# The sums for the adaLN gates in another stage, the third product's first operands split at another place, and residual rows and results by other times and queues

## Chip, cores, metric

The kernel runs on one core of one Trainium2 chip. The metric is the device time of one execution in microseconds, as the median of several; a profile shows one execution, taken by itself.

## What is computed

One step of a one-layer encoder over 2048 prompt tokens and 32 sample tokens of width 1024, all in fp32. The part of the reference that matters here:

```
mod = silu(c) @ w_ada + b_ada
shift, scale, gate = split(mod, 3)
h = rms_norm(x, norm_g) * (1 + scale) + shift
... = h @ w_in                       # q, k, v, za, index, u, bg, cg, zb, ga, gb
o = sparse_attention(...)            # top 256 keys of each query
a_out = (o * silu(za)) @ w_pa
b_out = (bg * y_conv * silu(zb)) @ w_pb
merged = sigmoid(ga) * a_out + sigmoid(gb) * b_out
y = x + gate * (merged @ w_out)
```

`gate` is one row of 1024 for the prompt and one for the sample tokens: a product of silu(c) with the last third of w_ada (`w_g` here, eight blocks of 128x1024, 512 KB each), done by VectorE as sums along a row.

## The kernel before

Products of fp32 numbers are made of two halves each: `split` casts an operand on ScalarE (ACT) to its high part, and VectorE (DVE) subtracts that from it for the low part (L173, L174); TensorE then does three matmuls. `wh`/`wl` are the parts of weights, `xh`/`xl` those of the other operand. The program is written for a tile framework; a scheduler sets the order of instructions on each engine from a simulated time, and `keep_in_program_order` binds single instructions to the order of the code. Each engine then executes strictly in that order, SyncE's (SP) queue of DMAs included.

The attention runs from about 1785 to 2363 us. Beside it goes a list of side work, `sum_steps`: sums of blocks of weights and pieces of the conv branch for the output stage, each with a cost, of which so many are done after each attention block as the block's share of the total asks for. At the end of that list stands `gates` (L1189): for each of the two rows it loads the row `c_d` to all partitions, loads the eight blocks of w_g (L1203, through the tiles `wq`), multiplies and sums each on DVE (L1206, `cgt`), adds the bias (L1210), and stores both results to `g_d` in DRAM (L1212), 4 KB each in pieces of 4 bytes.

The output stage `outputs` (L1451) does 64 products in the order of STEPS. For each of three groups of tokens (384, 384 and 256 + 16 columns) come b0 to b6 (conv branch), a0 to a6 (attention branch) and m0 to m6 (w_out): seven products of a Strassen-like scheme, where a matrix product of 2x2 blocks costs seven products of halves and some additions. A b or a product (`feature_step`, L1614 to L1616) has 48 matmuls of 384 (272) columns, an m product (`token_step`, L1678 to L1680) 72 of 256; in group 2 `sample_part` (L1636 to L1638) adds the sample tokens, whose split operands are `smh` and `sml`. After the matmuls of product n the code splits the operands of n+1 (`w_split`, `x_split`) and loads weights (`rw`, two of 512 KB) and pieces (`xq`, 768 KB) for n+3. Products 0 to 2 of each seven are copied out of PSUM by ACT (L1571), 3 to 6 added on DVE (L1575) and multiplied by the branch's gates `g` (L1583); a finished block of branch a is added to that of branch b (L1591), and so is an operand of the m products. `sums_a` (L1527 to L1530) makes differences of these blocks: q00 and t1, of which t1 is the operand of m1, and q01, that of m2. `ENDS` gives the block that products 3 to 6 finish; that of a6 is the operand of m3.

The products m3 to m6 load the residual rows into tiles `x` (L1670, six buffers, 128 KB a load) at their own start, multiply by the adaLN gate (L1686), add the rows (L1687) and store the result (L1689), all loads and stores on SP's queue. The gate tile itself is loaded at the stage's start from `g_d` (L1552).

## Time and profile before

| | |
|---|---|
| median of 3 runs | 2910.27 us (2905.02 to 2916.78) |
| profiled execution | 2908.65 us, its span 2906.9 us |
| PE busy in the span | 2788.8 us (96%), mean granted clock 0.986 |
| DVE, ACT, POOL busy | 2208.4 (76%), 1488.3 (51%), 924.2 us (32%) |
| DMA | 561.36 MB, mean 193 GB/s |
| output stage | from 2363.66 us on |

TensorE (PE) is the engine to look at: outside its busy time lie some 118 us of the span, and the rows below show which of them stand around the places that the change touches. In lists of waits a line reads "engine line waited for: us in total, times, longest us". In timelines the bracket at a line's end is the idle time of that engine before the instruction and what ended it. In windows, "PEclk" is the granted TensorE clock as a share of full speed, "DMA share" the busy share of the 16 DMA engines.

### The profile page before, as it was taken

To read this page: it belongs to the slowest core of one execution; us is meant where nothing else is said; L and a number is where in the kernel's file an instruction comes from. 1 tells how busy PE (TensorE), PEld (TensorE's weight loads), DVE (VectorE), ACT (ScalarE), POOL (GpSimd) and SP (SyncE) were. 2 spreads that over 40 slices of the span, in tenths; PEclk is the share of its full clock that TensorE was granted. 3 is DMA by queue.
4 is the path that set the end of the run, shared out by engine and by line. 5 is a ranking of instruction groups with operands and counts; after the bars stand their busy time and mean duration, and the time that the engine had idled before them with its cause. 6 is when DMAs were issued, how large, how long until landed. Compare 5 with 4: busy or idle time off the path is not lost. (4 is left out here: it accounts for less than half of the span.)

```text
span 2906.9 us, 53619 instructions
## 1 busy us (share of the span) xinstructions
PE 2788.8 (96%) x18925; PEld 2691.5 (93%) x18925; DVE 2208.4 (76%) x4948; ACT 1488.3 (51%) x2861; POOL 924.2 (32%) x1364
## 2 busy tenths in 40 slices
PE   7999999999999999999999999899999979999998
PEld 4999998999989999999999999889999879999997
DVE  5666576767664779999997878787777856888787
ACT  4434334666545665565553444555555544444453
POOL 2324223645544522222232222675544210000000
PEclk9999999999999999999999999999999999999999
DMA  7525567545554556555667666576555568596684
GB/s 255 179 92 184 158 218 242 191 147 171 167 179 161 164 178 204 186 180 185 208 212 226 203 223 170 143 209 179 170 161 158 169 194 301 189 292 220 216 296 142
DMA packets 469040, 561.36 MB, mean 193 GB/s; under 512 B 175584, under 2 KB 357272, under 8 KB 467736
## 3 DMA queue, kind: packets, MB, share of 16 engines
q1 hardware_dynamic: 464056, 553.57, 60.5%
q10 hardware_dynamic: 4704, 4.26, 0.4%
q8 instruction: 151, 2.47, 0.4%
q14 instruction: 129, 1.06, 0.1%
HBM read 373.34 MB, written 190.66 MB: 194 GB/s over the span
## 5 line engine op out<-in xcount | busy, mean ns | idle before, releaser
L975 PE MATMUL pm<-bh,wo 128*128 128x352 f32 (+1 forms) x2352 | 754.0, 322 | 2.7 <-ACT ev L987 1.2
L976 PE MATMUL pm<-bl,wo 128*128 128x352 f32 (+1 forms) x2352 | 753.2, 320 | 0.1
L977 PE MATMUL pm<-bh,wo 128*128 128x352 f32 (+1 forms) x2352 | 752.4, 321 | 0.0
L975 PEld LDWEIGHTS pm<-bh,wo 128*128 128x128 f32 x2352 | 442.7, 188 | 9.8 <-ACT ev L987 1.9
L976 PEld LDWEIGHTS pm<-bl,wo 128*128 128x128 f32 x2352 | 442.9, 188 | 5.7 <-DVE bl L174 0.6
L977 PEld LDWEIGHTS pm<-bh,wo 128*128 128x128 f32 x2352 | 442.0, 188 | 4.9 <-issue 0.5
L174 POOL TENSOR_TENSOR wo<-wr,wo 128x512 fp32r<-128x512 f32 x140 | 208.3, 1488 | 579.0 <-ACT wo L173 562.1
L745 PE MATMUL pm<-wh,hhi 128*128 128x256 f32 (+4 forms) x1088 | 309.5, 287 | 9.5 <-DVE sm L719 4.3
L746 PE MATMUL pm<-wl,hhi 128*128 128x256 f32 (+4 forms) x1088 | 307.5, 285 | 0.8 <-DVE wl L174 0.8
L747 PE MATMUL pm<-wh,hlo 128*128 128x256 f32 (+4 forms) x1088 | 306.4, 285 | 0.5 <-DVE hlo L174 0.5
L173 ACT CAST wh<-rw 128x1024 fp32r<-128x1024 f32 x128 | 134.1, 1051 | 211.9 <-PE ps L1615 83.3
L234 DVE SCALAR_TENSOR_TENSOR sc<-pi,wi,sc 128x512 f32<-128x512 f32 (+3 forms) x287 | 192.1, 670 | 55.0 <-ACT pi L230 51.6
L174 DVE TENSOR_TENSOR wl<-rw,wh 128x1024 fp32r<-128x1024 f32 x128 | 156.4, 1224 | 92.8 <-ACT wh L173 92.5
L173 ACT CAST th<-pt 128x512 fp32r<-128x512 f32 (+1 forms) x288 | 155.5, 562 | 137.0 <-PE pt L1380 124.0
L230 ACT ACTIVATE pi<-pi 128x512 f32<-128x512 f32 (+3 forms) x328 | 164.4, 516 | 118.8 <-PE pi L229 113.5
L1614 PE MATMUL ps<-xh,wh 128*128 128x384 f32 (+1 forms) x672 | 215.0, 323 | 9.7 <-ACT xh L173 5.6
L1615 PE MATMUL ps<-xl,wh 128*128 128x384 f32 (+1 forms) x672 | 216.1, 323 | 3.6 <-DVE xl L174 3.6
L1616 PE MATMUL ps<-xh,wl 128*128 128x384 f32 (+1 forms) x672 | 214.5, 322 | 0.7 <-DVE wl L174 0.7
L745 PEld LDWEIGHTS pm<-wh,hhi 128*128 128x128 f32 (+1 forms) x1088 | 200.0, 185 | 12.6 <-issue 5.1
L174 DVE TENSOR_TENSOR tl<-pt,th 128x512 fp32r<-128x512 f32 (+1 forms) x288 | 183.8, 656 | 35.2 <-ACT th L173 34.2
L746 PEld LDWEIGHTS pm<-wl,hhi 128*128 128x128 f32 (+1 forms) x1088 | 200.3, 185 | 2.4 <-issue 0.9
L747 PEld LDWEIGHTS pm<-wh,hlo 128*128 128x128 f32 (+1 forms) x1088 | 199.6, 184 | 1.8 <-DVE hlo L174 0.7
(307 smaller groups left out, 7151.2 us busy)
## 6 DMA issues: line engine op xcount, KB each, us to landing
u<-u_d SPq DMA_DIRECT2D x112, 520.0 KB, 4.4
wr<-in_w_f_dram SPq DMA_DIRECT2D x84, 512.0 KB, 3.8
rw<-o_d SPq DMA_DIRECT2D x72, 512.0 KB, 5.4
u_d<-ev SPq DMA_DIRECT2D x168, 176.0 KB, 2.2
rw<-in_w_q_dram SPq DMA_DIRECT2D x56, 512.0 KB, 5.3
wr<-in_w_t_dram SPq DMA_DIRECT2D x32, 512.0 KB, 4.7
xa_d<-a SPq DMA_DIRECT2D x64, 256.0 KB, 4.0
s_d<-ws SPq DMA_DIRECT2D x56, 256.0 KB, 2.9
```

The source lines that it names most:

```text
L173: S.copy(hi, src)
L174: (eng or V).tensor_tensor(lo, src, hi.bitcast(F32), ALU.subtract)
L234: V.scalar_tensor_tensor(sc[:n, o:o + w], pi[:n, :w], wi[:n, b, h:h + 1], sc[:n, o:o + w], ALU.mult, ALU.add)
L745: T.matmul(pm[:n, :ncol], a, hi[:, kt, :ncol], start=(kt == 0), stop=False)
L746: T.matmul(pm[:n, :ncol], a, lo[:, kt, :ncol], start=False, stop=False)
L747: T.matmul(pm[:n, :ncol], b_, hi[:, kt, :ncol], start=False, stop=(kt == KT - 1))
L975: T.matmul(ps[:, :tb], wh[:, kt, :], bh[:, kt, :tb], start=(first and kt == 0), stop=False, **more)
L976: T.matmul(ps[:, :tb], wh[:, kt, :], bl[:, kt, :tb], start=False, stop=False, **more)
L977: T.matmul(ps[:, :tb], wl[:, kt, :], bh[:, kt, :tb], start=False, stop=(kt == 3), **more)
L1614: T.matmul(ps[:, :tb], wh[:, kt, wc], xh[:, kt, :tb], start=(first and kt == 0), stop=False, **more)
L1615: T.matmul(ps[:, :tb], wh[:, kt, wc], xl[:, kt, :tb], start=False, stop=False, **more)
L1616: T.matmul(ps[:, :tb], wl[:, kt, wc], xh[:, kt, :tb], start=False, stop=(kt == 3), **more)
```

## The change

`gates` and its place at the end of the side list are gone. In the output stage the gate tile first holds the two rows of `c_d`. Halves of w_g's blocks (128x512, 256 KB, each loaded once) come by GpSimd's queue into pairs of the `x` tiles, three pairs ahead, and DVE sums each half with both rows (32 instructions of 128x512), three halves behind each of the products b0 to b2 and a0 to a2 of group 0. After a2 `gate_rows` adds the bias, stores to `g_d` and loads the gate tile from it on SP, as before. The operands of m0 are split behind a5, together with those of a6. The addition of a6's block and the difference q01 come behind m0, and the instructions around m1 are bound to the code's order. Residual rows are loaded one product ahead, and results are stored by GpSimd's queue, but for the last product's.

```diff
-        def gates():
...
-                    tc.keep_in_program_order(V.tensor_tensor_reduce(st["w"], st["w"], st["c"], 1.0, 0.0, ALU.mult, ALU.add, cgt[:, v, i:i + 1]))
...
-        return steps + gates()
+        return steps
...
+            def osplit(hi, lo, src, keep):
+                S.copy(hi, src)
+                ins = V.tensor_tensor(lo, src, hi.bitcast(F32), ALU.subtract)
+                if keep:
+                    tc.keep_in_program_order(ins)
...
-                V.tensor_tensor(t1[:, :, :tb], q11, q00, ALU.subtract)
-                V.tensor_tensor(q01, q11, q01, ALU.subtract)
+                tc.keep_in_program_order(V.tensor_tensor(t1[:, :, :tb], q11, q00, ALU.subtract))
+
+            def sums_c(g):
+                tb = GROUPS[g][1]
+                q01, q11 = [quads[g, "m", k][:, :, :tb] for k in QS[1:3]]
+                tc.keep_in_program_order(V.tensor_tensor(q01, q11, q01, ALU.subtract))
...
-            load(gate, g_d.rearrange("(o v) d -> o v d", o=1).broadcast_to([P, 2, D]))
+            cgt = oc.tile([P, 2, KT, 2], F32, name="cgt")
+            gws = {}
+
+            def gate_load(u):
+
+                if u < 2 * KT:
+                    gws[u] = xtile(), xtile()
+                    G.dma_start(gws[u][0], w_g[u // 2, :, 512 * (u % 2):512 * (u % 2) + 512])
+
+            def gate_sum(u):
+                w, t = gws.pop(u)
+                i, h = u // 2, u % 2
+                for v in range(2):
+                    V.tensor_tensor_reduce((t, w)[v], w, gate[:, v, 512 * h:512 * h + 512], 1.0, cgt[:, v, i, 0:1] if h else 0.0, ALU.mult, ALU.add,
+                                           cgt[:, v, i, h:h + 1])
+
+            def gate_rows():
+                g1 = cgt[:, :, :, 1]
+                V.scalar_tensor_tensor(g1, vecs[:, 16:24].unsqueeze(1).to_broadcast([P, 2, KT]), 0.25, g1, ALU.mult, ALU.add)
+                for v in range(2):
+                    store(g_d[v].rearrange("(k p) -> p k", p=P), cgt[:, v, :, 1])
+                load(gate, g_d.rearrange("(o v) d -> o v d", o=1).broadcast_to([P, 2, D]))
...
-                if j > 2:
+                if j > 2 and (jb, j) != ("a", 6):
                     gated(g, jb, j)
...
+            def rows_load(n):
+                g, jb, j = STEPS[n]
+                if jb == "m" and 2 < j < 7:
+                    resid[n] = [xtile() for _ in range(GROUPS[g][1] // P)]
+                    for i, x in enumerate(resid[n]):
+                        for q in range(2):
+                            load(x[64 * q:64 * q + 64], x_prompt[0][rows(n, i, q)])
...
-                                store(y_p[0][rows(i, q)], o[64 * q:64 * q + 64])
+                                (G.dma_start if n + 1 < len(STEPS) else store)(y_p[0][rows(n, i, q)], o[64 * q:64 * q + 64])
...
+            for v in range(2):
+                load(gate[:, v], c_d[v:v + 1].broadcast_to([P, D]))
+            for u in range(3):
+                gate_load(u)
+            units = list(range(2 * KT))
             for n, (g, jb, j) in enumerate(STEPS):
                 (token_step if jb == "m" else feature_step)(n)
                 wop.pop(n)
-                w_split(n + 1)
-                x_split(n + 1)
+                m0 = jb == "a" and j == 6
+                if not m0:
+                    w_split(n + 1)
+                    x_split(n + 1)
+                if jb == "a" and j == 5:
+
+                    w_split(n + 2)
+                    x_split(n + 2)
                 w_load(n + 3)
                 x_load(n + 3)
-                if jb == "a" and j == 6:
+                if n + 1 < len(STEPS):
+                    rows_load(n + 1)
+                if g == 0 and jb != "m" and j < 3:
+                    for u in units[:3]:
+                        gate_sum(u)
+                        gate_load(u + 3)
+                    units[:3] = []
+                    if jb == "a" and j == 2:
+                        gate_rows()
+                if m0:
                     sums_a(g)
+                if jb == "m" and j == 0:
+                    sums_c(g)
+                    gated(g, "a", 6)
```

On SP's queue, from the attention's last store of `a` on, before: loads of w_g, b3's weights (`rw_29615`, `rw_29617`), branch gates `g`, the store of the sums and residual rows `x` stand in one row.

```order
L1203 DMA wq_28882<-in_w_g_dram 128x1024
L1403 DMA xa_d<-a_29476 128x8x64
L1203 DMA wq_28885<-in_w_g_dram 128x1024
L1488 DMA rw_29615<-in_w_q_dram 128x2x512
L1514 DMA g_29621<-gb_d 128x4x768
L1212 DMA g_d<-cgt 128x8x1 x2
L1514 DMA g_29694<-gb_d 128x4x768
L1670 DMA x_30872<-in_x_prompt_dram 64x512 x2
L1488 DMA rw_29617<-in_w_q_dram 128x2x512
L1670 DMA x_30875<-in_x_prompt_dram 64x512
L1488 DMA rw_29688<-o_d 128x2x512
L1670 DMA x_30875<-in_x_prompt_dram 64x512
```

The same place after:

```order
L1369 DMA xa_d<-a_29420 128x8x64
L1706 DMA gate<-c_d 128x1024 x2
L1486 DMA g_29591<-gb_d 128x4x768
L1486 DMA g_29679<-gb_d 128x4x768
L1460 DMA rw_29570<-in_w_q_dram 128x2x512
L1460 DMA rw_29572<-in_w_q_dram 128x2x512
L1480 DMA xq_29750<-xb_d 128x4x384
L1460 DMA rw_29658<-o_d 128x2x512
L1480 DMA xq_29843<-xb_d 128x4x384
L1460 DMA rw_29660<-o_d 128x2x512
L1480 DMA xq_29922<-xa_d 128x4x384
```

The rows `c_d` and the branch gates now come first, b3's weights (`rw_29570`, `rw_29572`) stand together, and nothing of w_g, `g_d` or `x` is left there. The store of the sums and the gate's load now stand further down, between the two halves of a6's weights (`rw_30392`, `rw_30394`) and the first residual rows:

```order
L1460 DMA rw_30309<-o_d 128x2x512
L1660 DMA x_30902<-in_x_prompt_dram 64x512 x2
L1660 DMA x_30903<-in_x_prompt_dram 64x512
L1460 DMA rw_30392<-in_w_q_dram 128x2x512
L1660 DMA x_30903<-in_x_prompt_dram 64x512
L1548 DMA g_d<-cgt 128x8x1 x2
L1460 DMA rw_30394<-in_w_q_dram 128x2x512
L1660 DMA x_31017<-in_x_prompt_dram 64x512 x2
L1660 DMA x_31018<-in_x_prompt_dram 64x512
L1549 DMA gate<-g_d 128x2048
L1660 DMA x_31018<-in_x_prompt_dram 64x512
```

On DVE at the change from attention to output stage, before (the last three sums of w_g; `wl_29604` and `wl_29677` are weights of b1 and b2):

```order
L1398 TENSOR_TENSOR a_29476<-z_29474,po_29345 128x256
L1206 ISA wq_28882,cgt<-wq_28882,wq_28689 128x1024
L1206 ISA cgt 128x1
L174 TENSOR_TENSOR wl_29677<-rw_29542,wh_29676 128x1024
L1206 ISA wq_28885,cgt<-wq_28885,wq_28689 128x1024
L1206 ISA cgt 128x1
L1210 SCALAR_TENSOR_TENSOR cgt<-vecs,cgt 128x16
L174 TENSOR_TENSOR wl_29604<-rw_29536,wh_29603 128x1024
L174 TENSOR_TENSOR wl_29608<-rw_29538,wh_29607 128x1024
L174 TENSOR_TENSOR xl_29612<-xq_29534,xh_29611 128x1536
L174 TENSOR_TENSOR xl_29685<-xq_29540,xh_29684 128x1536
```

The same place after, where the sums (L1541) begin behind the splits of b1 and stand between those of b2 and b3:

```order
L1364 TENSOR_TENSOR a_29420<-z_29418,po_29289 128x256
L1443 TENSOR_TENSOR wl_29559<-rw_29480,wh_29558 128x1024
L1443 TENSOR_TENSOR wl_29563<-rw_29482,wh_29562 128x1024
L1443 TENSOR_TENSOR xl_29567<-xq_29478,xh_29566 128x1536
L1443 TENSOR_TENSOR wl_29647<-rw_29486,wh_29646 128x1024
L1541 ISA x_29493,cgt<-x_29492,gate 128x512
L1541 ISA cgt 128x1
L1443 TENSOR_TENSOR xl_29655<-xq_29484,xh_29654 128x1536
L1541 ISA x_29492,cgt<-x_29492,gate 128x512
L1541 ISA cgt 128x1
L1443 TENSOR_TENSOR wl_29651<-rw_29488,wh_29650 128x1024
L1443 TENSOR_TENSOR xl_29743<-xq_29574,xh_29742 128x1536
```

No sum stands ahead of b1's splits any more; the first stands ahead of the split of b2's piece (`xl_29655`).

On DVE between the last gates of group 0's a6 and the split of m3's operand, before (`xl_30680` is m1's, split from t1 = `xq_30589`; `ob_29708` is a6's block):

```order
L1591 TENSOR_TENSOR ob_29635<-ob_29635,oa_30157 128x1536
L1583 SCALAR_TENSOR_TENSOR oa_30230<-g_30216,ps_30111 128x384
L174 TENSOR_TENSOR wl_30676<-rw_30517,wh_30675 128x1024
L1527 TENSOR_TENSOR ob_29559<-ob_29635,ob_29559 128x1536
L1591 TENSOR_TENSOR ob_29708<-ob_29708,oa_30230 128x1536
L174 TENSOR_TENSOR wl_30764<-rw_30584,wh_30763 128x1024
L1529 TENSOR_TENSOR xq_30589<-ob_29858,ob_29559 128x1536
L1530 TENSOR_TENSOR ob_29635<-ob_29858,ob_29635 128x1536
L174 TENSOR_TENSOR xl_30864<-ob_29708,xh_30863 128x1536
L174 TENSOR_TENSOR wl_30768<-rw_30586,wh_30767 128x1024
L174 TENSOR_TENSOR xl_30680<-xq_30589,xh_30679 128x1536
```

The same place after (`xl_30708` is m1's, from t1 = `xq_30618`; `ob_29693` is a6's block):

```order
L1588 TENSOR_TENSOR ob_29605<-ob_29605,oa_30172 128x1536
L1580 SCALAR_TENSOR_TENSOR oa_30254<-g_30240,ps_30111 128x384
L1499 TENSOR_TENSOR ob_29514<-ob_29605,ob_29514 128x1536
L1501 TENSOR_TENSOR xq_30618<-ob_29858,ob_29514 128x1536
L1443 TENSOR_TENSOR wl_30700<-rw_30557,wh_30699 128x1024
L1443 TENSOR_TENSOR wl_30704<-rw_30559,wh_30703 128x1024
L1443 TENSOR_TENSOR wl_30794<-rw_30613,wh_30793 128x1024
L1443 TENSOR_TENSOR xl_30708<-xq_30618,xh_30707 128x1536
L1506 TENSOR_TENSOR ob_29605<-ob_29858,ob_29605 128x1536
L1588 TENSOR_TENSOR ob_29693<-ob_29693,oa_30254 128x1536
L1443 TENSOR_TENSOR wl_30798<-rw_30615,wh_30797 128x1024
L1443 TENSOR_TENSOR xl_30802<-ob_29605,xh_30801 128x1536
```

The addition of a6's block (L1591, now L1588), q01 (L1530, now L1506) and the splits for m3 moved from the front of m1's split to behind it.

## Rows read from the trace of the kernel before

**Rows 1.** The list of waits, TensorE only, from 2300 to 2907 us: who waited for whom, us in total, times, longest.

```profile
PE ps L1678 <- ACT xh L173: 8.5, 2, 4.2
PE ps L1614 <- ACT xh L173: 5.6, 2, 3.9
PE ps L1614 <- ACT ob L1571: 4.0, 1, 4.0
PE po L1388 <- DVE a L1398: 3.7, 2, 2.2
PE ps L1615 <- DVE xl L174: 3.6, 1, 3.6
PE ps L1636 <- ACT smh L173: 2.2, 1, 2.2
...
PE ps L1638 <- DVE sml L174: 1.8, 1, 1.8
```

**Rows 2.** Windows of the output stage: busy us (x instructions) of each engine, granted clock, DMA share, GB/s.

```profile
2370.00:2390.00 20.00, 14.65 (x72) 14.01 (x71) 11.49 (x11) 10.20 (x12) 0.00 (x0) 0.83 0.75 167
2400.00:2420.00 20.00, 16.13 (x71) 15.84 (x70) 8.97 (x10) 5.88 (x8) 0.00 (x0) 0.76 1.05 319
2510.00:2520.00 10.00, 6.28 (x30) 5.99 (x31) 8.59 (x6) 4.89 (x5) 0.00 (x0) 0.66 1.00 380
2690.00:2710.00 20.00, 15.61 (x108) 15.11 (x107) 14.03 (x10) 9.99 (x12) 0.00 (x0) 0.83 0.63 224
2830.00:2840.00 10.00, 10.00 (x81) 9.84 (x80) 10.00 (x23) 4.82 (x7) 0.00 (x0) 1.00 0.35 117
2840.00:2860.00 20.00, 15.93 (x113) 14.55 (x113) 17.62 (x25) 9.14 (x12) 0.00 (x0) 0.83 0.42 131
```

**Rows 3.** Windows of the attention's end and of group 0's b and a products, the same columns.

```profile
2300.00:2330.00 30.00, 25.95 (x190) 23.40 (x188) 25.76 (x49) 17.12 (x25) 6.13 (x13) 1.00 0.70 225
2330.00:2363.50 33.50, 29.15 (x227) 27.72 (x228) 21.99 (x39) 14.02 (x22) 5.74 (x13) 0.95 0.65 219
2414.70:2442.60 27.90, 27.82 (x146) 27.85 (x147) 26.81 (x37) 11.79 (x11) 0.00 (x0) 0.90 0.92 316
2442.60:2467.60 25.00, 25.00 (x146) 25.00 (x145) 13.48 (x12) 14.94 (x21) 0.00 (x0) 1.00 0.85 311
2467.60:2500.90 33.30, 33.30 (x195) 33.30 (x195) 32.13 (x42) 12.97 (x13) 0.00 (x0) 1.00 0.42 135
```

**Rows 4.** The instructions of line L1206, the sums over w_g: durations in ns (min/median/max), and what their engine waited for ahead of them (us, times).

```profile
L1206 DVE CUSTOM_DVE_ANT_0 wq<-wq,wq x16: 1214/1226/1279, 2277.1 to 2372.9; 128x1024 f32<-128x1024 f32 x16
...
  DMA wq<-in_w_g_dram: 11.7, 7
```

**Rows 5.** The list of waits, SP's queue only, from 2270 to 2425 us.

```profile
SPq L1203 <- DVE cgt L1206: 24.4, 7, 4.7
```

**Rows 6.** Timeline of SP's queue, start and duration of an issue.

```profile
2374.33 3.73 SPq L1212 DMA_DIRECT2D g_d<-cgt  x2
...
2380.93 4.14 SPq L1670 DMA_DIRECT2D x<-in_x_prompt_dram  x2
```

**Rows 7.** The view of the DMAs from 2360 to 2400 us: GB/s in 40 slices of one microsecond, then groups of issues with KB of each and median us from issue to landing.

```profile
GB/s 208 281 295 0 0 41 319 175 219 41 180 328 176 141 198 315 397 403 297 169 33 0 6 44 46 52 25 68 114 350 390 415 324 219 305 258 236 268 252 240
...
g<-gb_d SPq DMA_DIRECT2D x2, 1536.0 KB, 16.1
wq<-in_w_g_dram SPq DMA_DIRECT2D x3, 512.0 KB, 3.6
xq<-xb_d SPq DMA_DIRECT2D x2, 768.0 KB, 11.2
...
g_d<-cgt SPq DMA_DIRECT2D x2, 4.0 KB, 12.3
```

**Rows 8.** Timeline of ACT in the stage's start.

```profile
2397.16 1.04 ACT L173 CAST wh<-rw 128x1024 fp32r<-128x1024 f32 x1 [10.38 <-DMA rw<-in_w_q_dram]
```

**Rows 9.** Timeline of DVE ahead of group 0's m1.

```profile
2504.46 1.75 DVE L1591 TENSOR_TENSOR ob<-ob,oa 128x1536 f32<-128x1536 f32 x1
...
2507.27 1.75 DVE L1529 TENSOR_TENSOR xq<-ob,ob 128x1536 f32<-128x1536 f32 x1
```

**Rows 10.** Timeline of ACT at the same place.

```profile
2509.24 1.47 ACT L173 CAST xh<-ob 128x1536 fp32r<-128x1536 f32 x1 [0.73 <-PE ps L1679]
...
2512.05 1.47 ACT L173 CAST xh<-xq 128x1536 fp32r<-128x1536 f32 x1
```

**Rows 11.** Groups of DVE's instructions by line and shape over the whole span: count, busy us, mean ns of one, idle time before them.

```profile
L174 DVE TENSOR_TENSOR wl<-rw,wh 128x1024 fp32r<-128x1024 f32 x128 | 156.4, 1224 | 92.8 <-ACT wh L173 92.5
...
L1355 DVE CUSTOM_DVE_ANT_0 s<-ps,mk 128x512 f32<-128x512 f32 x32 | 21.8, 688 | 10.9 <-PE ps L1346 10.6 <-PE pt L1380 0.2
...
L1355 DVE DVE_READ_ACCUMULATOR2_ANT sc<- 128x1 f32 x232 | 19.6, 84 | 0.0
```

**Rows 12.** The instructions of line L1670, the residual rows' loads: durations of the issue in ns, who waited for them (us, times), us to landing.

```profile
L1670 SPq DMA_DIRECT2D x<-in_x_prompt_dram x64: 465/594/3554, 2380.9 to 2896.0; - x64
...
  DVE om L1687: 1.7, 1
...
DMA to landing us min/median/max: 2.6/4.6/13.8
```

More of the change, by code (lines that the diff above doesn't have):

```diff
@@ L158, in body @@
     cg = cp.tile([P, 2, KT], F32, name="cg")
-    cgt = cp.tile([P, 2, KT], F32, name="cgt")
     onec = cp.tile([P, 1], F32, name="onec")
@@ L1187, in unit @@
             return get, [(0.85, lambda a=a: add(*a)) for a in ops], put
-        def gates():
-            st = {}
-            gt = []
-            def row(v):
-                def get():
-                    st["c"] = tile_()
-                    load(st["c"], c_d[v:v + 1].broadcast_to([P, D]))
-                return get
-            def part(v, i):
-                def get():
-                    st["w"] = tile_()
-                    load(st["w"], w_g[i])
-                def dot():
-                    tc.keep_in_program_order(V.tensor_tensor_reduce(st["w"], st["w"], st["c"], 1.0, 0.0, ALU.mult, ALU.add, cgt[:, v, i:i + 1]))
-                return get, dot
-            def put():
-                V.scalar_tensor_tensor(cgt, vecs[:, 16:24].unsqueeze(1).to_broadcast([P, 2, KT]), 0.25, cgt, ALU.mult, ALU.add)
-                for v in range(2):
-                    store(g_d[v].rearrange("(k p) -> p k", p=P), cgt[:, v])
-            steps = []
-            for v in range(2):
-                steps.append((0.0, row(v)))
-                for i in range(KT):
-                    get, dot = part(v, i)
-                    steps += [(0.0, get), (1.2, dot)]
-            return steps + [(0.0, put)]
         units = [pieces(i) for i in range(32)] + [sample()]
@@ L1497, in w_split @@
                     hi, lo = [(oa, oc)[t // 2].tile([P, 4, 256], F32R, name=nm(x), tag=f"{x}{t}") for x in ("wh", "wl")]
-                    split(hi, lo, wraw.pop((n, i)).rearrange("p h (k c) -> p (h k) c", k=2))
+                    osplit(hi, lo, wraw.pop((n, i)).rearrange("p h (k c) -> p (h k) c", k=2), STEPS[n][1:] == ("m", 1))
                     wop[n].append((hi, lo))
@@ L1546, in x_split @@
                 hi, lo = [(ob if t == 0 else oc).tile([P, 4, TQ], F32R, name=nm(x), tag=f"{x}{t}") for x in ("xh", "xl")]
-                split(hi[:, :, :tb], lo[:, :, :tb], src[:, :, :tb])
+                osplit(hi[:, :, :tb], lo[:, :, :tb], src[:, :, :tb], (jb, j) == ("m", 1))
                 xop[n] = hi, lo
             gate = oc.tile([P, 2, D], F32, name="gate")
-            load(gate, g_d.rearrange("(o v) d -> o v d", o=1).broadcast_to([P, 2, D]))
+            cgt = oc.tile([P, 2, KT, 2], F32, name="cgt")
[16 more added lines that the diff above has]
+                load(gate, g_d.rearrange("(o v) d -> o v d", o=1).broadcast_to([P, 2, D]))
             smh = oc.tile([P, KT, NS], F32R, name="smh")
@@ L1590, in gated @@
                     a = out(g, "b", f, hf)
-                    V.tensor_tensor(a[:, :, :tb], a[:, :, :tb], o[:, :, :tb], ALU.add)
+                    ins = V.tensor_tensor(a[:, :, :tb], a[:, :, :tb], o[:, :, :tb], ALU.add)
+                    if j == 6:
+                        tc.keep_in_program_order(ins)
                     quads[g, "m", (f, hf)] = a
@@ L1646, in sample_part, with rows @@
                     store(y_s[0][:, fs_], y[:NS])
+            def rows(n, i, q):
+                g, _, j = STEPS[n]
+                f, hf = ENDS[j]
+                r0 = GROUPS[g][0] + (2 * i + q) * P + 64 * hf
+                return slice(r0, r0 + 64), slice(512 * f, 512 * f + 512)
+            def rows_load(n):
[5 more added lines that the diff above has]
+                            load(x[64 * q:64 * q + 64], x_prompt[0][rows(n, i, q)])
             def token_step(n):
@@ L1658, in token_step @@
                 first = j in (0, 3, 4)
-                xs = []
-                def rows(i, q):
-                    r0 = t0 + (2 * i + q) * P + 64 * hf
-                    return slice(r0, r0 + 64), slice(512 * f, 512 * f + 512)
                 if j > 2:
                     f, hf = ENDS[j]
-                    for i in range(nt):
-                        xs.append(xtile())
-                        for q in range(2):
-                            load(xs[i][64 * q:64 * q + 64], x_prompt[0][rows(i, q)])
+                    xs = resid.pop(n)
                 for c in range(2):
```

3 lines of the change are left out of this document (1 added, 2 removed).

## The prediction

> **What bounds the kernel now.** I read the list of TensorE's waits from 2300 us on first, because TensorE is busy nearly all the time and every microsecond it stands is paid in full. The list has four places in it [rows 1]: the end of the attention (a L1398, 3.7 us), the start of the output stage (L1614 and L1615: 5.6 + 4.0 + 3.6 = 13.2), m1 in groups 0 and 1 (L1678, 8.5 in two waits of 4.2), and the sample tokens' part of group 2 (L1636 and L1638, 2.2 + 1.8 = 4.0). Then the windows around these places [rows 2]. An undisturbed stretch, a0 to a2 of group 0, does 146 matmuls of 384 columns in 25.00 us, 0.171 each [rows 3]. After a stall the granted clock is lower and matmuls that count as busy take longer: in 2370 to 2390, 72 matmuls need 12.3 us and took 14.65; in 2400 to 2420, 71 need 12.1 and took 16.13. So the stage's start pays 2.3 + 4.0 = 6.3 us beside its 13.2 of standing still.
>
> Then why. At the stage's start DVE ends the sixteen sums over w_g, for whose loads it has stood 11.7 us in all [rows 4], while SP, whose loads wait for the buffers of these sums, has waited 24.4 us for DVE [rows 5]. SP then issues the store of the gate sums, 3.73 us, and residual rows that nothing needs before m3, 4.14 us for two [rows 6], ahead of half of b4's weights. In the slices of one microsecond from 2380 to 2388 the traffic falls to 0 to 68 GB/s [rows 7]; in the same list the two stores of 4 KB take 12.3 us to land. ACT then stands 10.38 us for weights [rows 8], and TensorE behind it.
>
> **The change part by part.** The sum stands against the profiled execution's own 2908.65 us (its span of 2906.9 and 1.75 around it); the median of the three runs is 1.6 above.
>
> *The sums leave the attention.* 16 x (1.23 + 0.08) = 21 us of DVE [rows 4, 11] and 8 MB of loads go from its last 90 us. There TensorE stands 30.00 - 25.95 = 4.05 us in 2300 to 2330 and 33.50 - 29.15 = 4.35 in 2330 to 2363.5 [rows 3], 3.7 of the 8.4 on DVE's a. I take about half: **-4**. The list of side sums is shorter, so those that stay are paced later, into this stretch, and the scheduler arranges it anew: bounds -8 and +4.
>
> *The start of the output stage.* The store of the sums, the gate's load and 12 residual row loads (1.5 MB) go from it. In come c_d rows and w_g halves. By the sizes of the transfers [rows 7], up to b3 SP and GpSimd must bring 1 MB of c_d rows, 3 of branch gates, 1 of b3's weights and 0.75 of halves, 5.75 MB; each product more takes 1 of weights, up to 1.5 of pieces and 0.75 of halves: 9 MB up to b4, 12.3 up to b5. At the 319 GB/s of 2400 to 2420 [rows 2] that is 18, 28 and 38.5 us. A product takes 48 x 0.171 = 8.2 us, so b3, b4 and b5 start 25, 33 and 41 us after b0, and need 1.04 + 1.04 + 1.47 = 3.5 us of ACT's casts ahead [rows 8, 10]: the transfers are in time at b3, up to 1 us late at b5. Of the 13.2 us I keep 1.5 (the wait at b1, on ACT's order of copies and casts) and 3 for late weights, since the pieces' exact order is a scheduler's. Of the 6.3 us of clock about 4 come back: 13.2 - 4.5 + 4 = 12.7, **-13**; bounds -6 (all weights 2 us late from b4 on, the low clock stays) and -17.
>
> *m1's first operands early.* In before t1 is made at 2507.27, behind the addition of a6 at 2504.46 [rows 9], and ACT casts another product's operand at 2509.24 before t1's at 2512.05 [rows 10]. The order of the changed kernel puts q00 and t1 directly behind a5's addition, a6's after the split of m1, and q01 after it too. Two instructions of 1.75 us leave the queue in front of m1's split, which is more than half of the 4.2 us, and the other cast is behind. The matmuls slowed after the wait go too. Undisturbed, a 256-column one takes between two thirds of 0.171, 0.114, and the 10.00 / 81 = 0.123 of a window of group 2 with 272 columns [rows 2]; I take 0.117. In 2510 to 2520, 30 need 3.5 us and took 6.28; in 2690 to 2710, 108 need 12.6 and took 15.61: 2.8 and 3.0. Twice 7, less 1 for a wait on m1's xl in their place: **-13**, bounds -5 and -14. Splitting m0 at a5 is in itself worth nothing: no wait of TensorE stands at m0.
>
> *Group 2.* 4.0 us of waits, and of clock 15.93 - 113 x 0.117 = 2.7 in 2840 to 2860 [rows 2]. Splits of weights and a6's addition leave the queue in front of the samples' sml; the split of m1 follows it as closely as before while m1 may start earlier, so a wait of some 2.5 us can stand there: **-4**, bounds 0 and -6.
>
> *The end.* DVE waits 1.7 us for the last residual rows [rows 12], which are issued a product's end before their use; a step ahead they have landed: **-1.7**. Stores on GpSimd's queue: no wait of TensorE is on SP's stores, GpSimd is not busy in any window of the stage, and the last product's stay on SP: 0, bounds -1 and +2.
>
> *What it adds.* 32 sums of 128x512. The nearest rows are the attention's, 688 ns and 84 for reading the sum [rows 11]: 32 x 0.77 = 25 us of DVE. Eight stand before b3's first addition, where DVE waits for ACT and ACT for weights. 24, 18.5 us, fall into what was 2414.7 to 2500.9, where DVE is busy 26.81 of 27.90, 13.48 of 25.00 and 32.13 of 33.30 us [rows 3]: 13.8 us are free, nearly all in the middle one. The first of these stretches is dense because it works off what the stalls left. With b3 at its proper time, the order's instructions by the rows' durations give about 36 us of DVE for TensorE's 33 in b3 to b6, 22 for 25 in a0 to a2 and 30 for 33 in a3 to a6. So DVE is 3 us late at the end of b6 and catches up after it; splits stand a product ahead, which covers part: **+3.5**, bounds 0 and +10. The store of the sums now stands on SP between the two halves of a6's weights. What is queued behind it has two products, 16 us, to spare against 12.3: 0, bounds 0 and +8.
>
> Sum: -4 - 13 - 13 - 4 - 1.7 + 3.5 = -32.2, 2876.4 on the profiled execution; with the 1.6 to the median **2878**.
>
> **Rivals.**
>
> *VectorE waits for GpSimd's loads (slower).* Thirteen of the sixteen halves can be issued only when two sums have freed a pair of buffers, and DVE executes in order: a sum whose half is late holds back the splits that TensorE needs. Between a release and the sum that wants the new half the order leaves 8 to 16 us of DVE work (its instructions by the rows' durations), for the thirteenth and fourteenth half only 2.5 and 5, on the average 10. The trace has no DMA issued by GpSimd, so its landing is bounded by SP's: 2.6 us at least and 13.8 at most for 128 KB of residual rows [rows 12], 3.6 for 512 KB of the same matrix [rows 7]; of these the last is the nearest, and 5 to 7 in the crowded start is what I take. At L us the cost is 13 x (L - 10). It eats the whole gain at 12.5 and makes the kernel slower by 0.5% at 13.6. At 15 us: 2878 + 65 = **2943**. For it: in 2400 to 2420 the DMA share is 1.05, and rows then landed late. Against: part of that was the small store. Chance 0.10.
>
> One rule speaks for it. The Trainium skill, SBUF — State Buffer, section "SBUF: two separate sides", warns that a DMA issued from GpSimd's queue has its descriptors written by GpSimd's cores, and that these are locked out while VectorE runs an instruction in its two-port mode. By it each load would start later by up to one DVE instruction and this rival would come sooner. The rows have DVE's splits and sums at 1.2 to 1.3 ns an element, none at a faster pace, and no run here shows the lock.
>
> *The transfers bind the start.* The halves share the DMA engines with weights that are just in time; b3 to b6 are each about 3 us late and the low clock stays. The start then gives 2 instead of 13, and DVE, later by as much, leaves nothing of group 0's m1 (6.5): 2878 + 11 + 6.5 = **2895**. Chance 0.15.
>
> *The waits only move.* The attention's end, arranged anew, loses 4 instead of gaining 4, and m1 waits for xl or weights as long as it did for xh: 2878 + 8 + 13 = **2899**. Chance 0.12. That the change doesn't do what it says is left out, since the order shows it at all three places.
>
> **How the numbers follow.** The forecast, all its lower bounds together at 2862 and 12 us upward, has 0.63. A measurement of this kernel can tell about 0.5%, 14.5 us, from no change, so faster is below 2895.7. The second rival lies on that edge, half to each side; the third is within; the first is nearly all beyond 2924.8. Faster 0.71, same 0.20, slower 0.09. The range goes from 2862 to 2904, the third rival with some spread of its own, and leaves out the first.
>
> **What the profile will show.** Right: after b1 no wait of TensorE over 2 us until a0 and a clock near 1.0 from 2370 on; L1678's waits gone in groups 0 and 1; the sums at about 0.7 us; GpSimd's loads landing below 8 us; DVE without idle time around b5 and b6. Wrong: DVE idle ahead of the new sums, released by w_g (first rival); ACT idle before wh, released by rw, in b3 to b6 (second); TensorE waiting for xl at m1, or more idle time in the attention's last 60 us (third). The cheapest way to be wrong is the start, whose 13 us rest on traffic that I could only add up.

## The result, and the profile after

The changed kernel takes 2871.77 us, the median of 4 runs (2867.70 to 2877.02); the kernel before, on the same chip, 2908.59 (2905.02 to 2916.78). The ratio is 0.9871, with a 95% interval of 0.9844 to 0.9897: 1.3% faster. The forecast was 2878, its range 2862 to 2904.

The profiled execution took 2871.81 us, its span 2870.0. TensorE is busy 2775.9 us, 13 less than before for the same 18925 matmuls, and idle 94 us for 118: part of the gain is waits, part is matmuls that no longer run at a low clock.

The list of TensorE's waits from 2300 us on, to be read against [rows 1] (lines have moved: L1613 to L1615 are the b and a products, L1683 to L1685 the m products, L1355 the attention):

```profile
PE ps L1685 <- DVE xl L1443: 3.0, 2, 1.6
PE po L1355 <- DVE tl L173: 2.6, 2, 1.5
PE ps L1635 <- ACT wh L1442: 1.1, 1, 1.1
...
PE ps L1613 <- ACT wh L1442: 0.9, 2, 0.5
PE ps L1613 <- ACT oa L1568: 0.8, 1, 0.8
PE ps L1615 <- DVE wl L1443: 0.5, 1, 0.5
```

All the waits that the prediction named are gone; the longest is 1.6 us, a wait on xl at group 0's m1, as said. The windows, to be read against [rows 2, 3] (busy us and instructions of PE, PEld, DVE, ACT, POOL, then clock, DMA share, GB/s):

```profile
2300.00:2330.00 30.00, 28.62 (x225) 27.03 (x224) 21.65 (x40) 18.09 (x28) 15.08 (x24) 1.00 0.76 237
2330.00:2358.40 28.40, 25.81 (x196) 25.01 (x195) 15.94 (x26) 11.83 (x20) 3.73 (x10) 0.88 0.45 135
2358.40:2384.00 25.60, 25.25 (x146) 24.93 (x144) 16.17 (x22) 14.13 (x18) 5.21 (x10) 1.00 0.89 312
2384.00:2419.80 35.80, 34.49 (x193) 33.52 (x194) 34.61 (x60) 17.42 (x18) 3.28 (x6) 1.00 0.95 331
2419.80:2446.00 26.20, 25.27 (x143) 24.63 (x143) 23.91 (x39) 14.23 (x19) 1.64 (x3) 1.00 0.98 347
2488.00:2498.00 10.00, 8.31 (x64) 7.52 (x63) 10.00 (x8) 6.15 (x8) 0.00 (x0) 1.00 1.05 388
2669.00:2689.00 20.00, 19.80 (x166) 19.59 (x165) 15.68 (x12) 13.62 (x16) 0.00 (x0) 1.00 0.66 215
```

The first two are the attention's end: its idle time went from 8.4 to 1.4 + 2.6 us. From b0 on the granted clock is 1.00 in all of them, where it was 0.66 to 0.83 around the waits. In 2384 to 2419.8, b3 to b6, DVE is busy 34.61 of 35.80 us at a DMA share of 0.95: the part of the stage that now runs late. The sums and their loads, to be read against [rows 4, 12]:

```profile
L1541 DVE CUSTOM_DVE_ANT_0 x<-x,gate x16: 679/683/692, 2368.0 to 2445.6; 128x512 f32<-128x512 f32 x16
L1541 DVE CUSTOM_DVE_ANT_0 x<-x,gate,cgt x16: 739/744/750, 2373.7 to 2448.0; 128x512 f32<-128x512 f32 x16
...
  DMA x<-in_w_g_dram: 0.6, 1
```

```profile
L1535 POOL DMA_DIRECT2D x<-in_w_g_dram x16: 546/546/824, 2361.1 to 2431.7; - x16
...
  DVE cgt L1541: 62.1, 12
...
DMA to landing us min/median/max: 4.1/6.0/8.8
```

The sums take 0.68 and 0.74 us, as estimated. GpSimd's loads land in 4.1 to 8.8 us, 6.0 in the median: the median is inside the 5 to 7 that the prediction took, the slowest above the 8 that it named as a sign. DVE stood for one of them, 0.6 us. What GpSimd waits for, 62.1 us, costs nothing: its queue holds nothing else. In the view of the DMAs from 2440 to 2480 us (slices of one microsecond) the hole of [rows 7] has moved with the store behind a2, to 2454 to 2463, where 20 GB/s are moved at a DMA share of 0.67 (2380 to 2388 before: 34 GB/s, 0.67):

```profile
GB/s 380 389 383 385 389 354 176 266 279 281 215 223 267 113 15 0 0 35 33 25 29 14 27 117 354 318 262 352 403 268 229 291 275 309 385 385 328 168 317 107
```

The stretches below are differences between the starts of products' first matmuls in TensorE's timeline, in us; "end" is the span's end.

| stretch | before | after | change |
|---|---|---|---|
| attention, its last twelve half blocks | 168.5 | 164.5 | -4.0 |
| group 0, b0 to b3 | 38.16 | 25.81 | -12.35 |
| b3 to a0 | 40.48 | 35.61 | -4.87 |
| a0 to m0 | 58.24 | 60.14 | +1.90 |
| m0 to m3 | 32.68 | 28.36 | -4.32 |
| group 1, b0 to m0 | 116.48 | 117.52 | +1.04 |
| m0 to m3 | 32.71 | 25.61 | -7.10 |
| group 2, m0 to m3 | 26.69 | 21.18 | -5.51 |
| m6 to the end | 16.72 | 17.57 | +0.85 |
| all from b0 to the end | 543.24 | 511.62 | -31.62 |

The attention's beginning and everything before it varies by several us from one execution to the next, in unchanged code too, so parts of the change are best compared by such stretches. They are of one profiled execution each. The changed kernel was profiled a second time, below: its stage is 2.1 us longer there, all of it in group 0's m0 to m3.

The stretch from m6 to the end has two parts. From m6's first matmul to the end of VectorE's last sum it is 8.9 us, 10.5 before; from there to the span's end 8.7, 6.2 before. In that last part GpSimd's queue executes a DRAIN, an instruction at the end of an engine's program, of 6.28 us, of which the lists of waits say nothing. It ends 1.15 us before the span does, and GpSimd's signal to the other engines follows it; SP's own DRAIN ended 2.0 us earlier. The instructions of that line, first of the changed kernel, then of the kernel before (ns min/median/max, first and last start in us):

```profile
L1859 POOLq DRAIN  x3: 40/107/6277, 2862.6 to 2869.7; - x3
```

```profile
L1832 POOLq DRAIN  x3: 34/50/82, 2370.3 to 2906.6; - x3
```

### The profile page after: what moved, and what is told of

Same layout as the page of the kernel before. It is cut to its first block, busy times and chain, and to the rows that moved or that the text cites. A ratio compares the mean times of both kernels' runs of the same rounds, so it can differ in the third digit from the quotient of the medians.

```text
span 2870.0 us, 53720 instructions
## 1 busy us (share of the span) xinstructions
PE 2775.9 (97%) x18925; PEld 2681.0 (93%) x18925; DVE 2211.0 (77%) x4980; ACT 1485.8 (52%) x2861; POOL 965.5 (34%) x1440
## 5 line engine op out<-in xcount | busy, mean ns | idle before, releaser
L1613 PE MATMUL ps<-xh,wh 128*128 128x384 f32 (+1 forms) x672 | 214.1, 321 | 2.1 <-ACT wh L1442 0.9
L1615 PE MATMUL ps<-xh,wl 128*128 128x384 f32 (+1 forms) x672 | 211.9, 320 | 0.5 <-DVE wl L1443 0.5
```

Of the source, the lines that this page charges most:

```text
L1613: T.matmul(ps[:, :tb], wh[:, kt, wc], xh[:, kt, :tb], start=(first and kt == 0), stop=False, **more)
L1615: T.matmul(ps[:, :tb], wl[:, kt, wc], xh[:, kt, :tb], start=False, stop=(kt == 3), **more)
```

## The experiments

Twelve kernels ran, in three sets, each set beside the kernel before on the same chip. The table at the end of this section has their stretches.

**One part alone: the sums.** The changed kernel with the two other parts undone:

```diff
-                if not m0:
-                    w_split(n + 1)
-                    x_split(n + 1)
-                if jb == "a" and j == 5:
-
-                    w_split(n + 2)
-                    x_split(n + 2)
+                w_split(n + 1)
+                x_split(n + 1)
...
-                if n + 1 < len(STEPS):
-                    rows_load(n + 1)
...
-                if jb == "m" and j == 0:
-                    sums_c(g)
-                    gated(g, "a", 6)
```

> The kernel before with one part of the change: the sums for the gates go from the attention into the output stage (halves of w_g by GpSimd's queue, store and gate load behind a2); m1 is split as before, residual rows are loaded at their own product, results stored by SP. The prediction's terms for this part are -4 (attention), -13 (start) and +3.5 (the sums on VectorE), -13.5 together; read from the changed kernel's trace they are -8 and -15.6, some -24 together. If this part alone clears SP and the DMA queues at the stage's start: 2884 to 2895 us, the waits of L1678 at m1 still there at about 4 us each. If the start is late because of the residual rows and not of the sums: 2900 or more, with idle ACT before weights in b3 to b5.

Measured 2900.94 us beside 2914.43, ratio 0.9950 (0.9933 to 0.9967): 13.5 us less, what the prediction's terms say, not the 24 read from the changed kernel. The agreement in the sum is partly luck. The start is as short as in the changed kernel, 61.5 us from b0 to a0 and 17.1 less than before, so the residual rows are not what makes it late. But 4.4 us are given back from m0 to m3 of group 0 (37.1 for 32.7; TensorE waits 5.0 us for xh and 3.1 for xl there), 3.2 from a0 to m0, 2.0 in group 1's b and a products and 3.0 in group 2's. The profiled execution, 2906.30 us, was the slowest of the eight.

**One part alone: m1.** The changed kernel with sums, rows and stores as before:

```diff
-        return steps
+        return steps + gates()
...
+            load(gate, g_d.rearrange("(o v) d -> o v d", o=1).broadcast_to([P, 2, D]))
...
-                if g == 0 and jb != "m" and j < 3:
-                    for u in units[:3]:
-                        gate_sum(u)
-                        gate_load(u + 3)
```

> The kernel before with one part of the change: m0 split behind a5, t1 and m1's split ahead of the addition of a6's block and of q01, pinned in the code's order; sums for the gates in the attention as before, rows and stores as before. By the prediction -13 (groups 0 and 1) and -4 (group 2): 2891 us, L1678's waits gone, the start's stalls as before. By the rival (the wait only moves to xl or weights at m1): within 5 us of before.

Measured 2894.92, ratio 0.9938 (0.9916 to 0.9960). TensorE's waits from 2300 to 2890 us:

```profile
PE ps L1626 <- ACT xh L1476: 4.9, 2, 3.1
PE ps L1626 <- ACT ob L1581: 4.6, 1, 4.6
...
PE ps L1627 <- DVE xl L1477: 3.6, 1, 3.6
...
PE ps L1699 <- DVE xl L1477: 1.3, 1, 1.3
```

The waits at the start (L1626, L1627) stand as before; at m1 (L1697 to L1699) 1.3 us on xl are left of the 8.5. m0 to m3 takes 26.4 and 25.6 us in groups 0 and 1 and 21.3 in group 2, so 6.3 + 7.1 + 5.4 = 18.8 are gained: the term and its place are right, and the wait did not move to weights. The b and a products of groups 1 and 2 give back 1.6 each.

**One part alone: rows and stores.** The kernel before with:

```diff
-                    for i in range(nt):
-                        xs.append(xtile())
-                        for q in range(2):
-                            load(xs[i][64 * q:64 * q + 64], x_prompt[0][rows(i, q)])
+                    xs = resid.pop(n)
...
-                                store(y_p[0][rows(i, q)], o[64 * q:64 * q + 64])
+                                (G.dma_start if n + 1 < len(STEPS) else store)(y_p[0][rows(n, i, q)], o[64 * q:64 * q + 64])
...
+                if n + 1 < len(STEPS):
+                    rows_load(n + 1)
```

> The kernel before with one part of the change: residual rows loaded one product ahead, results stored by GpSimd's queue except the last product's. By the prediction -1.7 at the end and nothing else, since the first twelve row loads have nothing to wait for and stand in SP's queue at the stage's start as before: 2905 to 2909 us. If the rows' new place in the code takes them out of the start: 2895 or less.

Measured 2911.67, ratio 0.9990 (0.9979 to 1.0001): 2.8 us less by the medians, not clear of no change. From m6 to the end 1.0 us went, from b0 to a0 1.3. As said; the loads still stand in the start, since nothing there makes them wait.

**The store later.** The kernel before, sums and rows where they were, the store and the gate tile's load pinned behind a2:

```diff
-            return steps + [(0.0, put)]
+            return steps
...
+                for v in range(2):
+                    tc.keep_in_program_order(store(g_d[v].rearrange("(k p) -> p k", p=P), cgt[:, v]))
+                tc.keep_in_program_order(load(gate, g_d.rearrange("(o v) d -> o v d", o=1).broadcast_to([P, 2, D])))
...
+                if (g, jb, j) == (0, "a", 2):
+                    gate_rows()
```

> The kernel before, its sums for the gates still in the attention, but the store of 4 KB twice and the gate tile's load are pinned on SP behind the loads that follow a2; residual rows still stand in the start. If it is the small store that starves the start (traffic of 0 to 68 GB/s for eight microseconds): the stalls at b2 to b4 go, 10 to 15 us less, 2894 to 2899 us, with the low traffic now behind a2. If it is the sums with their waits and the residual rows: within 4 us of before.

Measured 2909.22, ratio 0.9984 (0.9972 to 0.9995): by the total 5 us less, between the two that were expected, but the stretches say more. b2 falls from 13.64 to 8.32 us and b3 to a0 from 40.5 to 33.3, 12.7 us for the start. Where the store now stands, 5.8 of these come back: a0 to m0 +3.0, m0 to m3 +2.8. The view of the DMAs from 2435 to 2475 us, slices of one microsecond:

```profile
GB/s 326 263 260 307 213 255 298 316 401 403 400 380 192 49 1 0 14 25 20 14 23 39 212 335 395 424 412 410 447 442 415 351 402 401 404 412 406 393 176 57
```

From 2448 to 2457 the traffic is 0 to 49 GB/s: the hole goes with the store. So the store is the larger part of the start's loss, and a move alone carries nearly half of it elsewhere. The residual rows still stand in this start, and b3 to a0 takes what four products at 8.32 us take, 33.3: they cost nothing there. b0 to b2 stays at 24.3 us: that part belongs to the sums.

**The store in larger pieces.** The kernel before, with the 16 x 128 sums transposed by TensorE and stored as 16 rows of 512 bytes:

```diff
-                for v in range(2):
-                    store(g_d[v].rearrange("(k p) -> p k", p=P), cgt[:, v])
+                pt = acc(1)
+                tc.keep_in_program_order(T.transpose(pt[:2 * KT, :P], cgt.rearrange("p v k -> p (v k)"), ident))
+                gr = xtile()
+                V.tensor_copy(gr[:2 * KT, :P], pt[:2 * KT, :P])
+                store(g_d.rearrange("v (k p) -> (v k) p", p=P), gr[:2 * KT, :P])
...
+                if (g, jb, j) == (0, "b", 2):
+                    gate_rows()
```

> The kernel before, sums for the gates still in the attention, but their results are transposed by TensorE and stored as 16 rows of 512 bytes, behind b2, instead of 2048 pieces of 4 bytes. m1 and the rest as before. The fourth kernel of the first set showed 65.9 us from b0 to a0 (before 78.6) with the small store behind a2, and gave some 6 us back there. If the pieces are the cause of the low traffic: the start is as short or shorter, 61 to 66 us, no slices of 0 to 68 GB/s, and a3 and m0 to m2 are as in the kernel before; 2896 to 2901 us. If any store and reload of the gates at this place delays the weights: 70 us or more from b0 to a0.

Measured 2900.53, ratio 0.9945 (0.9929 to 0.9960); 66.1 us from b0 to a0, and a0 to m0 at 58.2 and m0 to m3 at 33.5 as before. The traffic from 2371 to 2411 us:

```profile
GB/s 201 320 152 123 33 270 301 195 139 297 415 415 421 412 424 412 421 404 387 402 398 399 406 403 404 401 401 405 411 374 400 387 398 222 212 275 311 215 381 346
```

No hole: some 400 GB/s for twenty microseconds. The pieces of 4 bytes are the cause, not the store nor its place. The stage of this profiled execution is 10.4 us shorter than before, 12.6 of it in the start and 2.2 given back elsewhere.

**The same in the changed kernel,** with the transpose behind a3.

> The changed kernel with the sums transposed by TensorE behind a3 and stored as 16 rows of 512 bytes. In the changed kernel the traffic is low for nine microseconds behind a2 and m2 of group 0 takes 11.03 us where group 1's takes 9.10. If that is the price of the small pieces: m2 near 9.1, the low slices gone, 2 us less, about 2870 us. If m2 is late because VectorE is: m2 stays above 10.5 us.

Measured 2871.38 beside 2915.67, ratio 0.9846 (0.9832 to 0.9859). What the expectation calls m2 is the stretch from m1's first matmul to m2's; it fell from 11.03 to 9.02 us, m0 to m3 from 28.36 to 26.10, and the stage by 2.3 to 509.4.

**The sums alone, with larger pieces** (one execution), to learn what the first kernel gave back:

> The first kernel of the first set (only the sums moved, m1 as before) with the sums stored as 16 rows of 512 bytes behind a3. That kernel took 38.9 us from m0 to m3 of group 0, the kernel before 33.0. If the small pieces behind a2 are the cause, by weights that land late: 33 to 34 us, and the stage 534 us or less. If VectorE's sums make it late for m1: 36 us or more.

2889.59 us, the stage 530.1. From m0 to m3 it takes 31.5 us, where the first kernel took 37.1 and the kernel before 32.7. (The 38.9 and 33.0 of the expectation run from a6's first matmul to m2's; by that count it is 32.0.) The wait that is left there is the old one at m1:

```profile
PE ps L1675 <- ACT xh L172: 4.2, 1, 4.2
```

So the first kernel's loss there was the hole, not the sums.

**Halves on SP's queue** (one execution):

```diff
-                    G.dma_start(gws[u][0], w_g[u // 2, :, 512 * (u % 2):512 * (u % 2) + 512])
+                    load(gws[u][0], w_g[u // 2, :, 512 * (u % 2):512 * (u % 2) + 512])
```

> The changed kernel with one edit: the sixteen halves of w_g are loaded by SP's queue and not by GpSimd's. In the changed kernel GpSimd's queue stands 62.1 us in twelve waits for VectorE's sums to free the buffers; on SP the same waits stand ahead of weights. If GpSimd's queue is what keeps the weights on time: b3 to b6 and a0 to a2 become late by 10 us or more together, 2880 us or more. If the transfers bind the start and not the queues: within 4 us of the changed kernel's 61.4 us from b0 to a0.

2871.76 us, the stage 506.0: 60.9 from b0 to a0 and 58.8 from a0 to m0. The loads land in 10.5 us in the median (6.0 from GpSimd), DVE waits 4.0 us for three of them, and SP 9.4 us for DVE, and no stretch of the table gets longer by more than 0.2 us. GpSimd's queue is not what gave the gain. Why a0 to m0 gets 1.4 us shorter by it isn't shown.

**Results on SP's queue** (one execution): the changed kernel with `store(y_p...)` throughout.

> The changed kernel with one edit: all results are stored by SP's queue. By the prediction nothing: the m products' lengths within 0.3 us each and the stage's length, 511.6 us in the changed kernel, within 2 us. By a rival in which SP's stores, which wait for VectorE, hold back weights behind them: 4 us or more longer, in the products behind m3 to m6.

2879.06 us, the stage 514.6, 3.0 longer. From m3 to the next group's b0, where most of the stores are, it takes what it took (34.4 us), but the b and a products of groups 1 and 2 took 0.9 and 1.9 more, and group 0's m0 to m3 30.4 for 28.4, ahead of the first store. The unedited changed kernel, run again below, took 30.5 there, so that part is its own spread. From m6 to the end it is 2.3 us shorter: GpSimd's DRAIN takes 1.38 us here and stands at 2443.6, far from the end. One execution doesn't settle whether SP's stores hold back weights for 1 to 3 us of the next products.

**Both edits** in the changed kernel: larger pieces and halves on SP.

> The changed kernel with two edits: sums transposed and stored as 16 rows of 512 bytes behind a3, and the halves of w_g loaded by SP's queue. Each alone shortened the stage, from 511.6 us to 509.4 (rows) and 506.0 (SP's queue, one look). If the two gains are separate: 504 to 507 us from b0 to the span's end, about 2866 us. If both come from the same place, the weights behind a2: 506 to 509 us, the same as one alone.

**And the sums spread**, one half behind each of b0 to b6 and three behind each of a0 to a2, pinned:

```diff
-                if g == 0 and jb != "m" and j < 3:
-                    for u in units[:3]:
+                if g == 0 and jb != "m" and (jb == "b" or j < 4):
+                    k = 1 if jb == "b" else 3
+                    for u in units[:k]:
```

> The kernel of this set's first entry with the sums pinned and spread: one half behind each of b0 to b6, three behind each of a0 to a2, so that fewer bytes and less of VectorE's work lie in b3 to b6. In the changed kernel b3 to a2 of group 0 take 62.4 us where seven at 8.32 take 58.2. If the halves' bytes and sums are the cause: b3 to a2 at 60 us or less, some 2 us less than the first entry. If the weights, pieces and gates alone bind the start: no shorter.

**And the changed kernel once more,** on their chip:

> The changed kernel itself, unedited, for a comparison on the same chip with the two kernels above: 0.985 to 0.989 of the kernel before, a stage of 510 to 513 us, m2 of group 0 near 11 us.

Beside 2910.67 of the kernel before: the changed kernel 2872.13 (0.9876, 0.9856 to 0.9897), with both edits 2865.07 (0.9851, 0.9834 to 0.9869), with the sums spread as well 2864.35 (0.9849, 0.9829 to 0.9870). The runs of the last two (2861.57 to 2868.17 and 2861.50 to 2867.07) all lie below those of the first (2869.65 to 2875.68), so both are some 7 us better than the changed kernel; between the two the times tell nothing. The stage is 505.2 us with both edits, 6.5 less than in the changed kernel, where the two alone gave 2.3 and 5.6, by one execution each. The 1.4 us that they would share is less than the 2.1 by which the changed kernel's own two executions differ. In the traces, spreading shortens b3 to a3 from 61.4 to 58.8 us, where seven products at 8.32 take 58.2, and m0 to m3 takes 1.5 us more. In the windows from b3 to a0 of the first and of the second TensorE idles 2.0 us and not at all:

```profile
2383.00:2418.80 35.80, 33.77 (x192) 33.13 (x191) 34.23 (x61) 17.01 (x16) 0.00 (x0) 1.00 0.97 340
```

```profile
2383.00:2416.60 33.60, 33.60 (x194) 33.60 (x193) 32.28 (x54) 15.29 (x14) 0.00 (x0) 1.00 0.99 351
```

The changed kernel's second profile has m0 to m3 of group 0 at 30.5 us, where the first has 28.4. TensorE's wait on xl at m1 is 1.6 us in both, but here the granted clock fell around it, and 1.6 of the 2.1 us lie between m1's first matmul and m2's. The window around the wait, to be read against that of 2488 to 2498 in the first profile, which has 64 matmuls in as long a time and a clock of 1.00:

```profile
2487.00:2497.00 10.00, 7.81 (x47) 7.03 (x46) 10.00 (x8) 5.66 (x7) 0.00 (x0) 0.83 1.05 385
```

The stretches of all twelve, of one profiled execution each:

| us | b0 to b3 | b3 to a0 | a0 to m0 | m0 to m3 | group 1, m0 to m3 | group 2, m0 to m3 | m6 to end | stage |
|---|---|---|---|---|---|---|---|---|
| sums alone | 25.73 | 35.79 | 61.45 | 37.11 | 32.42 | 26.73 | 17.37 | 539.22 |
| m1 alone | 39.21 | 39.53 | 58.24 | 26.36 | 25.64 | 21.30 | 17.00 | 527.57 |
| rows alone | 38.52 | 38.77 | 58.24 | 32.93 | 32.89 | 25.62 | 15.68 | 539.63 |
| store later | 32.66 | 33.28 | 61.25 | 35.43 | 32.61 | 25.72 | 16.43 | 536.63 |
| before, 512-byte rows | 32.70 | 33.37 | 58.24 | 33.46 | 33.16 | 26.72 | 16.66 | 532.80 |
| sums alone, 512-byte rows | 25.87 | 35.62 | 60.26 | 31.53 | 32.75 | 26.17 | 16.67 | 530.14 |
| changed, halves on SP | 25.11 | 35.76 | 58.76 | 26.55 | 25.61 | 20.76 | 16.59 | 505.98 |
| changed, results on SP | 25.86 | 35.76 | 60.75 | 30.44 | 25.60 | 21.19 | 15.31 | 514.62 |
| changed, 512-byte rows | 25.55 | 35.76 | 60.27 | 26.10 | 25.61 | 21.17 | 17.44 | 509.36 |
| both edits | 25.11 | 36.08 | 58.88 | 26.11 | 25.61 | 21.09 | 15.71 | 505.16 |
| both, spread | 25.11 | 33.57 | 58.81 | 27.61 | 25.60 | 20.71 | 15.51 | 503.37 |
| changed again | 25.70 | 35.78 | 60.49 | 30.49 | 25.60 | 20.72 | 17.53 | 513.69 |

## Why the prediction was right, point by point

The sum was 4.6 us short (-32.2 forecast, -36.8 between the two profiled executions), and most of its terms are right in place and size. That it came so near is partly luck: the start and what the sums add came out 5.8 us better together than forecast, and m1, the end and group 1's b and a products 5.2 worse.

- *The attention's end, -4.* Right. Its last twelve half blocks took 167.6 to 171.6 us in five executions with the sums inside, 169.8 in the mean, and 161.8 to 166.1 in nine without, 164.1 in the mean: 5.7 apart.
- *The start, -13.* The mechanism is right, the size was low: b0 to a0 fell by 17.2. I had kept 1.5 us for a wait at b1, 3 for late weights and 2.3 of the clock. The wait at b1 went, the clock came back whole, and 3.2 us over seven products at 8.32 are left, in b2 to b6, at a DMA share near 1.0. They are not the late weights alone: TensorE stands 0.9 us of them for casts of weights that landed late (L1613 on wh) and 0.7 for VectorE (0.5 of it L1615 on wl), and with both edits and the sums spread 0.4 us are left in all. So they are mostly the same loss that I had put at +3.5 under the added sums; whether by the halves' bytes or by VectorE's work, no run tells apart. The experiments divide the gain: larger pieces alone give 12.6, of b2 and after, and the sums' leaving gives the 7.7 of b0 to b2, against some 3 that their new place costs.
- *m1, -13.* m0 to m3 fell by 4.3 and 7.1, together 11.4. Group 1 is as forecast. In group 0 some 2 us are missing by the hole behind a2: with larger pieces the wait of 1.6 us on xl is gone and 2.3 come back. The hole is not the only cause: with the halves on SP's queue it is there too, and 0.2 us of the wait are left.
- *Group 2, -4.* -5.5: the wait on m1's xl that I allowed 2.5 for was 1.4.
- *The end, -1.7.* The wait on the rows went: from m6 to VectorE's last sum 10.5 us became 8.9, as forecast. But the whole from m6 to the end is 0.85 longer, since 2.5 came up behind the last sum. The step that failed is "stores on GpSimd's queue: 0": I looked for waits of TensorE and for GpSimd's busy time, and left out what GpSimd does at its program's end when it has issued DMAs. Its DRAIN takes 6.28 us in the three executions where it issues both the 16 halves and 60 results, and SP has then been done for some 2 us; 4.97 us in the four where it issues the 60 results alone, which costs 0.3 us at most, since SP is done hardly earlier; and 1.38 us in the three with the halves alone, where it stands between 2438 and 2446 us. By these numbers it is an estimated 0.08 to 0.09 us for each DMA that GpSimd issued. From m6 on it is 17.4 to 17.6 us in the first three and 15.3 to 16.6 in the others that have the sums, m1 and the rows' loads changed together. What makes up the other 0.5 us wasn't followed.
- *The added sums, +3.5.* b3 to a0 has 2.3 over the 33.3 of the kernel without them there, a0 to m0 1.9; with the sums spread it is 0.3 and 0.6. VectorE is busy nearly all of b3 to b6, as said, but TensorE stands only 0.7 us for it there. Part of a0 to m0 goes with the two edits together (58.9); larger pieces alone leave it at 60.3.
- *The small store behind a2, 0 with bounds 0 and +8.* Mis-sized: up to 2.3 us, and some 2 more when the clock falls around the wait on xl, as in the second profile. The two products that I counted to spare cover most of it, not all.
- *Stores on GpSimd's queue, 0.* Wrong at the end, see there; during the stage no wait of TensorE came of them.

The rivals: VectorE never waited for GpSimd's loads as the first had it (0.6 us; they landed in 6.0, the break-even was 12.5). Of the Trainium skill's rule in SBUF — State Buffer, "SBUF: two separate sides", on descriptors locked out by VectorE's two-port mode, no run here shows an effect: GpSimd's sixteen issues took 0.55 us each in the median and 0.82 at most. That the same loads landed later from SP's queue, in 10.5 us for 6.0, doesn't test the rule, since they stand behind other loads there. The second rival, transfers that bind the start, holds for at most 3 us where it had 11. Its sign was there all the same: ACT stood 17.9 us for weights (rw) from 2358 to 2420, and TensorE behind it only 0.9, so ACT's idle time is no sign by itself. The third did not happen: of the waits at m1, 1.6 us in group 0 and 1.4 in group 2 are left, on xl.

## What to carry to other kernels

Look for a store or load of tiny pieces when the traffic falls to nothing while the DMA engines count as busy: two stores of 4 KB in 4-byte pieces cost the start 12.6 us here, moving them brought nearly half of that back in another place, and a transpose on TensorE took the hole away. What holds a stage's start back may be several things, one behind the other: test the pieces one by one. Compare stretches between fixed points of the trace to see where time went, but take the size of a part from the medians: in single profiled executions the three parts alone gave 4, 16 and 4 us of the stage and the whole 32, while by the medians they gave 13.5, 19.5 and 2.8, in sum 35.8 of the whole's 36.8. When DMAs move to another engine's queue, look at what that engine still does at the end of the kernel. When an in-order engine makes the operands of the next product, put the instructions that this product needs ahead of those that only a later one needs.

## What the runs showed of the hardware

- Two stores of 4 KB in pieces of 4 bytes hold the traffic at 0 to 68 GB/s for eight to eleven microseconds in all nine profiled executions that have them, wherever they stand in the stage, though loads are queued behind them; as 16 rows of 512 bytes they leave no such hole in five.
- Loads of 256 KB issued by GpSimd took 0.55 us each to issue and landed in 4.1 to 8.8 us at a DMA share of 0.89 to 0.98.
- GpSimd's DRAIN behind its last DMA took 1.38 us after 16 DMAs, 4.97 after 60 and 6.28 after 76, and at the end of the kernel the other engines waited for it.
- The granted clock around a wait is not the same each time. A wait of 1.6 us at m1 left it at 1.00 (2.4 GHz) in one execution of the changed kernel, and in another the mean of 2487 to 2497 us was 0.83, a mix of 1.2 and 2.4 GHz. Around waits of 1.8 to 4.2 us it was 0.66 to 0.83 in windows of the kernel before [rows 2].
- Group 1's seven b and seven a products take 117.5 us and more in the kernels with the sums in the output stage, and 116.5 in those without (but for m1 alone, 118.1), though the sums are in group 0. No wait of TensorE is behind the 1.0 us; in b5, for one, its matmuls start 173 to 182 ns apart for 173 to 174 before. Why is open.
